# Seven-product blocks in a two-layer decoder trunk: products combined in PSUM, the fourth weight sum from SBUF, none put off

## The chip, the cores and the metric

One core of one Trainium2 chip runs the whole program. The metric is device time in microseconds. The kernel before took 1740.78 us (median of 3 runs, 1734.89 to 1745.19).

## What is computed

512 tokens of width 1024 pass two layers. Each layer computes, in float32:

```python
h = rms_norm(x, g)
proj = h @ w_in            # 7168 columns: pool, ret q/k, ret v, ret gate, mem q, 3 branch gates
merged = g_pool * (y_pool @ w_up_pool) + g_ret * (y_ret @ w_up_ret) + g_mem * (y_mem @ w_up_mem)
x = x + merged @ w_out
h2 = rms_norm(x, g2)
x = x + square(relu(h2 @ w_mlp1)) @ w_mlp2      # 1024 -> 4096 -> 1024
```

Between `proj` and `merged` stand three mixers: a causal pooling mixer, a retention with four heads in chunks of 128 tokens, and an attention to 256 memory tokens. After the second layer follows a last `rms_norm`.

## The kernel before, in words

**Precision.** Every operand is split into a high and a low part in fp32r: ScalarE casts (`wh`, `xh`), VectorE subtracts (`wl`, `xl`). Each matrix product is three matmuls, high by high, high by low, low by high (`mm`, lines 119 to 125). Weights are split by `split_w` (L114 ScalarE, L117 VectorE), into four buffers of each kind.

**Sections.** The large matrices are cut to blocks of 1024 x 1024, 16 per layer. One call of `products` is one section: a block in 2 x 2 quarters of 512, by the Strassen-Winograd scheme with seven products in place of eight. Operand quarters are `x.q[i, j]` (i: half of the tokens or columns, j: half of the contraction), results are (0,0), (0,1), (1,1) and (1,0). Before, the order is 1, 2, 5, 3, 6, 7, 4. Products 1 and 2 give (0,0); (0,1) needs 1, 5, 6 and 3; (1,1) needs 1, 5, 6 and 7; (1,0) needs 1, 6, 7 and 4 (signs left out). Each product has two halves of the contraction, `kp` 0 and 1, called units here: 24 matmuls of 256 columns each where the result is stored features first (`fm`), 12 of 512 columns else.

**Sums.** Sums of operand quarters are made by VectorE (`Operand.value`, L267) and split (`Operand.get`, L104 and L105). Sums of weight quarters are made by DMA: `Weight.take` splits a raw buffer, then GpSimd adds the next quarter from HBM to it (L225, accumulating). Buffer A holds w00, then + w01, then + w11, then + w10; buffer C holds w10, and buffer B holds w11, then + w01. So 6 loads and 8 accumulating DMAs of 512 KB make one section's weights. Eight raw tiles are shared.

**Order.** `push` prepares a unit (weight split, operand parts) and issues the matmuls of the unit three places before (`LOOK`). After each unit `settle` runs what is due: the function `after` of the product that ended (results out of PSUM, `done` for the sections that store, `acc` for those that add to x at L1183), operand parts in `wanted`, and one step of each side task (`advance`: norms, transposes, retention, pooling, attention). TensorE's order is as issued; the other engines are ordered by a scheduler, which `urgent` overrides. `until` goes on with the queue, and with empty steps after it, until a side task has what the next section needs.

**The put-off product.** In all sections but those called with `last=True` (w_out and the layer's last MLP block), product 4 is kept in `late` and issued by `owed` in the next section, after that section's product 1, accumulating on product 7's banks. So result (1,0) comes out two products into the next section. Product 2 then accumulates on product 1's banks, whose contents ScalarE has copied to `u` (L346).

**The layer's end.** `flush` and `drain` stand inside the loop over layers: at the end of layer 0 the queue and the side tasks are emptied before the next layer's first unit is prepared.

Of the kernel before, what the change touches and what calls it, by code (L numbers as in the profile page):

```python
# [13 lines left out]
ALU = mybir.AluOpType  # L14
# [11 lines left out]
NT = T // P  # L26
# [42 lines left out]
def tile_trunk(ctx, tc, a, out):  # L69
# [71 lines left out]
    wanted = []  # L141

    def settle():

        nonlocal post
        if post:
            f, post = post, None
            f()
        for w in list(wanted):
            x, p, kp = w  # L150
            if x.have(p, kp):
                x.get(p, kp)
                wanted.remove(w)
        advance()
# [37 lines left out]
    class Weight:  # L192
# [21 lines left out]
        def take(self, p, kp, between=None):  # L214
# [5 lines left out]
            part, then = {1: ("A", q(0, 1)), 5: ("A", q(1, 1)), 6: ("A", q(1, 0)), 4: ("A", None),  # L220
# [22 lines left out]
    class Operand:  # L243
# [12 lines left out]
        def value(self, p, kp):  # L256
# [4 lines left out]
            if (p, kp) not in self.sums:  # L261
                x, y, op = {5: lambda: (q[1, 0], q[1, 1], ALU.subtract),
                            6: lambda: (self.value(5, kp), q[0, 0], ALU.subtract),
                            7: lambda: (q[0, 0], q[1, 0], ALU.subtract),
                            3: lambda: (q[0, 1], self.value(6, kp), ALU.add)}[p]()
# [12 lines left out]
    late = []  # L278
    early = {}

    def owed():
        while late:
            late.pop(0)()

    def products(x, done, fm=False, last=False, acc=None, ahead=None):
# [15 lines left out]
        follows = {1: 2, 2: 5, 5: 3, 3: 6, 6: 7, 7: 4}  # L301

        def prep(p, kp, w=w):
            def f():
                wp = w.take(p, kp)
                for q in (p or 1, follows.get(p)):
                    if q and x.have(q, kp):
                        x.get(q, kp)
# [7 lines left out]
        def go(p, kp, into, new, fm=fm, then=None):  # L316
            def f(wp):
# [17 lines left out]
                if kp == n - 1:  # L335
                    return lambda: urgent(after, p, into) if last and p == 4 else after(p, into)
# [3 lines left out]
        def after(p, into):  # L340
            v = nc.vector.tensor_tensor
            bs = range(2)
            if p == 1:
                for b in bs:
                    sb["u", b] = slot(name="u2")
                    nc.scalar.copy(sb["u", b], ps[1][b])  # L346
            elif p == 2:
                for b in bs:
                    if acc:
                        if into == 2:  # L350
                            acc(0, 0, b, sb["u", b], ALU.add, False)
                        acc(0, 0, b, ps[into][b], ALU.add, True)
                    elif into == 1:
                        done(0, 0, b, ps[1][b], True)
                    else:
                        c = slot(name="c11")
                        v(c, sb["u", b], ps[2][b], ALU.add)
                        done(0, 0, b, c, False)
            elif p == 5 and acc and last:
                for b in bs:  # L360
                    sb["v", b] = slot(name="vv")
# [927 lines left out]
```

## Time and profile before

| | |
|---|---|
| median of 3 runs | 1740.78 us |
| the profiled execution | 1739.72 us |
| its span, first to last instruction | 1737.9 us |
| mean granted TensorE clock | 0.975 |
| TensorE busy | 1638.8 us (94%) |
| VectorE busy | 1329.6 us (77%) |
| ScalarE busy | 949.1 us (55%) |
| GpSimd busy | 332.1 us (19%) |
| read from HBM | 288.56 MB |

The profile gives busy times of each engine, the share of the TensorE clock that was granted, and what ended each idle time. A clock of 1.00 is 2.4 GHz and of 0.5 is 1.2 GHz. Matmuls overlap, and their ends are modelled: the pitch from one start to the next tells more than the duration of one.

### The profile page before, as it was taken

To read this page: it belongs to the slowest core of one execution; us is meant where nothing else is said; L and a number is where in the kernel's file an instruction comes from. 1 tells how busy PE (TensorE), PEld (TensorE's weight loads), DVE (VectorE), ACT (ScalarE), POOL (GpSimd) and SP (SyncE) were. 2 spreads that over 40 slices of the span, in tenths; PEclk is the share of its full clock that TensorE was granted. 3 is DMA by queue.
4 is the path that set the end of the run, shared out by engine and by line. 5 is a ranking of instruction groups with operands and counts; after the bars stand their busy time and mean duration, and the time that the engine had idled before them with its cause. 6 is when DMAs were issued, how large, how long until landed. Compare 5 with 4: busy or idle time off the path is not lost. (4 is left out here: it accounts for less than half of the span.)

```text
span 1737.9 us, 24766 instructions
## 1 busy us (share of the span) xinstructions
PE 1638.8 (94%) x9354; PEld 1430.2 (82%) x9354; DVE 1329.6 (77%) x1833; ACT 949.1 (55%) x1463; POOL 332.1 (19%) x292
## 2 busy tenths in 40 slices
PE   6899998999998999999979999999999899999996
PEld 5797887988878897979769888889788797979794
DVE  4898674876698878787887786758667988786878
ACT  6445664555266645455663457645544565545563
POOL 2122202200012212222121222021001122222221
PEclk9999998999999999999989999999999899999998
DMA  9699985963667978889789999767455778888874
GB/s 267 143 218 261 233 218 107 189 187 111 187 137 152 188 177 170 178 173 188 180 183 203 221 262 223 202 122 176 144 167 141 167 148 191 193 164 179 174 136 101
DMA packets 163449, 311.17 MB, mean 179 GB/s; under 512 B 11320, under 2 KB 12544, under 8 KB 163328
## 3 DMA queue, kind: packets, MB, share of 16 engines
q0 software_dynamic: 69632, 134.23, 46.6%
q1 hardware_dynamic: 83872, 159.42, 28.1%
q10 hardware_dynamic: 9824, 15.93, 2.6%
q8 instruction: 73, 1.20, 0.3%
q14 instruction: 48, 0.39, 0.1%
HBM read 288.56 MB, written 16.78 MB: 176 GB/s over the span
## 5 line engine op out<-in xcount | busy, mean ns | idle before, releaser
L114 ACT CAST wh<-raw 128x1024 fp32r<-128x1024 f32 x496 | 519.6, 1050 | 600.6 <-PE P L125 192.8
L117 DVE TENSOR_TENSOR wl<-raw,wh 128x1024 fp32r<-128x1024 f32 x496 | 605.6, 1224 | 284.8 <-ACT wh L114 283.4
L225 POOL DMA_DIRECT2D raw<-in_w_mlp x124 | 149.8, 1210 | 473.7 <-DVE wl L117 455.3
L225 POOL DMA_DIRECT2D raw<-in_w_in x108 | 131.3, 1216 | 454.3 <-DVE wl L117 340.8
L123 PE MATMUL P<-wh,x3h 128*128 128x512 f32 x160 | 68.7, 430 | 15.1 <-ACT x3h L104 15.0
L125 PE MATMUL P<-wh,x3l 128*128 128x512 f32 x160 | 69.1, 432 | 8.9 <-DVE x3l L105 8.9
L225 POOL DMA_DIRECT2D raw<-in_w_out x16 | 19.3, 1207 | 295.3 <-DVE wl L117 282.7
L1183 DVE TENSOR_TENSOR x<-x,P 128x512 f32<-128x512 f32 x104 | 68.4, 684 | 6.6 <-PE P L125 6.1
L124 PE MATMUL P<-wl,x3h 128*128 128x512 f32 x160 | 67.0, 419 | 1.9 <-DVE wl L117 1.9
L124 PE MATMUL P<-wl,x4h 128*128 128x512 f32 x160 | 64.2, 402 | 3.9 <-DVE wl L117 3.9
L123 PE MATMUL P<-wh,x1h 128*128 128x512 f32 x160 | 64.7, 404 | 1.7 <-ACT x1h L104 1.7
L125 PE MATMUL P<-wh,x5l 128*128 128x512 f32 x160 | 65.1, 407 | 0.6 <-DVE x5l L105 0.6
L123 PE MATMUL P<-wh,x4h 128*128 128x512 f32 x160 | 64.1, 401 | 1.1 <-ACT wh L114 1.1
L123 PE MATMUL P<-wh,x5h 128*128 128x512 f32 x160 | 63.2, 395 | 1.7 <-ACT x5h L104 1.7
L124 PE MATMUL P<-wl,x1h 128*128 128x512 f32 x160 | 63.9, 400 | 0.0
L125 PE MATMUL P<-wh,x1l 128*128 128x512 f32 x160 | 63.7, 398 | 0.0
L125 PE MATMUL P<-wh,x4l 128*128 128x512 f32 x160 | 63.5, 397 | 0.0
L123 PE MATMUL P<-wh,x2h 128*128 128x512 f32 x160 | 63.2, 395 | 0.0
L124 PE MATMUL P<-wl,x6h 128*128 128x512 f32 x160 | 62.5, 391 | 0.6 <-DVE wl L117 0.6
L124 PE MATMUL P<-wl,x5h 128*128 128x512 f32 x160 | 63.0, 394 | 0.0
L124 PE MATMUL P<-wl,x7h 128*128 128x512 f32 x160 | 62.6, 391 | 0.4 <-DVE wl L117 0.4
L124 PE MATMUL P<-wl,x2h 128*128 128x512 f32 x160 | 62.9, 393 | 0.0
(331 smaller groups left out, 5140.8 us busy)
## 6 DMA issues: line engine op xcount, KB each, us to landing
raw<-in_w_mlp POOLq DMA_DIRECT2D x128, 512.0 KB, 6.5
raw<-in_w_in POOLq DMA_DIRECT2D x112, 512.0 KB, 6.8
raw<-in_w_mlp SPq DMA_DIRECT2D x100, 512.0 KB, 4.6
raw<-in_w_in SPq DMA_DIRECT2D x88, 512.0 KB, 4.9
sgl<-sig SPq DMA_DIRECT2D x48, 256.0 KB, 5.8
raw<-in_w_mem_kv SPq DMA_DIRECT2D x16, 512.0 KB, 4.9
raw<-in_w_up_ret SPq DMA_DIRECT2D x16, 512.0 KB, 4.6
raw<-in_w_out POOLq DMA_DIRECT2D x16, 512.0 KB, 6.6
```

Source lines behind the costliest of these rows:

```text
L114: nc.scalar.copy(hi, raw)
L117: nc.vector.tensor_tensor(lw, raw, hi.bitcast(F32), ALU.subtract)
L123: nc.tensor.matmul(ps, sh, mh, start=start, stop=False, skip_group_check=True)
L124: nc.tensor.matmul(ps, sh, ml, start=False, stop=False, skip_group_check=True)
L125: nc.tensor.matmul(ps, sl, mh, start=False, stop=stop, skip_group_check=True)
L225: nc.gpsimd.dma_start(raw, rows2(then, kp), accum_op=ALU.add)
L1183: nc.vector.tensor_tensor(x, x, part, op)
```

## The change

Order and combination: the order is now 1, 2, 5, 3, 6, 4, 7. After product 5 ScalarE copies its two banks onto those of product 2. Product 6 accumulates on product 5's banks, VectorE then subtracts `u` there, product 4 accumulates on the copy in product 2's banks, product 7 on product 5's. No product goes to the next section, and `late`, `owed` are gone; signs of three operand sums are turned. Weights: buffer A ends with three terms, and the fourth sum is buffer C plus buffer A, both in SBUF. The loads move: A after product 2, C after product 6. `flush` and `drain` come once, at the end of the program. Some side tasks take other numbers of steps.

```diff
+    follows = {1: 2, 2: 5, 5: 3, 3: 6, 6: 4, 4: 7}
...
-        for w in list(wanted):
-            x, p, kp = w
-            if x.have(p, kp):
-                x.get(p, kp)
-                wanted.remove(w)
+        had = [w for w in wanted if w[0].have(*w[1:])]
+        for w in had:
+            w[0].get(*w[1:])
+            wanted.remove(w)
+        for x, p, kp in had:
+            q = follows.get(p)
+            if q and x.have(q, kp):
+                x.get(q, kp)
...
-            part, then = {1: ("A", q(0, 1)), 5: ("A", q(1, 1)), 6: ("A", q(1, 0)), 4: ("A", None),
+            part, then = {1: ("A", q(0, 1)), 5: ("A", q(1, 1)), 6: ("A", None), 4: ("C", None),
                           3: ("B", q(0, 1)), 7: ("B", None), 2: ("C", None)}[p]
...
+            if (p, kp) in ((3, 1), (6, 0)):
+                k = 0 if p == 3 else 1
+                nc.gpsimd.dma_start(self.buf["C"][k], self.buf["A"][k], accum_op=ALU.add)
...
-                    return lambda: urgent(after, p, into) if last and p == 4 else after(p, into)
+                    return lambda: urgent(after, p) if p in (5, 6) or (last if p == 7 else not acc if p == 2 else False) else after(p)
...
+            elif p == 2 and acc:
+                for b in bs:
+                    acc(0, 0, b, ps[2][b], ALU.add, False)
+                for b in bs:
+                    acc(0, 0, b, sb["u", b], ALU.add, True)
...
+            elif p == 5:
                 for b in bs:
+                    nc.scalar.copy(ps[2][b], ps[5][b])
             elif p == 3 and acc:
                 for b in bs:
                     acc(0, 1, b, ps[3][b], ALU.add, False)
+                    if last:
+                        acc(0, 1, b, sb["u", b], ALU.subtract, False)
+            elif p == 6:
                 if last:
                     for b in bs:
+                        acc(0, 1, b, ps[5][b], ALU.add, True)
                 for b in bs:
+                    v(ps[5][b], ps[5][b], sb["u", b], ALU.subtract)
+                if acc and not last:
+                    for b in bs:
+                        acc(0, 1, b, ps[5][b], ALU.add, True)
+                elif not acc:
+                    cs = [slot(name="c12") for _ in bs]
+                    for b in bs:
+                        nc.scalar.copy(cs[b], ps[5][b])
+                    for b in bs:
+                        v(cs[b], cs[b], ps[3][b], ALU.add)
+                    for b in bs:
+                        done(0, 1, b, cs[b], False)
+            elif p == 4 and acc:
                 for b in bs:
+                    acc(1, 0, b, ps[2][b], ALU.add, False)
+            elif p == 7 and acc:
+                for i, op in ((1, ALU.add), (0, ALU.subtract)):
+                    for b in bs:
+                        acc(1, i, b, ps[5][b], op, True)
+            elif p == 7:
+                cs = [slot(name="c21") for _ in bs]
                 for b in bs:
+                    nc.scalar.copy(cs[b], ps[5][b])
                 for b in bs:
+                    v(cs[b], ps[2][b], cs[b], ALU.subtract)
                 for b in bs:
+                    done(1, 1, b, ps[5][b], True)
                 for b in bs:
+                    done(1, 0, b, cs[b], False)
...
+        if ahead:
+            product_ahead(*ahead)
+        product(2)
+        if nxt:
+            nxt.load("A")
         product(5)
         product(3)
-        product(6)
-        product(7)
+        product(6, 5)
+        if nxt:
+            nxt.load("C")
+        product(4, 2)
+        product(7, 5)
         if nxt:
             nxt.load("B")
-        if last:
-            product(4)
-        else:
-            late.append(lambda: product(4, 7))
...
-                transposed(x, i, c, kp, lambda t, c: xn[t % 2, c], g, eng=nc.vector if kp else None)
+                transposed(x, i, c, kp, lambda t, c: xn[t % 2, c], g)
...
-            vs = []
+            vs = [split(v[0][hp], name="vs")]
+            yield
+            yield
             for t in range(NT):
-                vs.append(split(v[t][hp], name="vs"))
-                yield
+                if t + 1 < NT:
+                    vs.append(split(v[t + 1][hp], name="vs"))
                 yield
                 yield
...
+            if h == 0:
+                yield
+                yield
...
-            yield
+            for _ in range(3):
+                yield
...
-        flush()
-        drain()
+    flush()
+    drain()
```

## Rows read from the trace of the kernel before

**Rows 1.** The page, busy time of each engine.

```profile
PE 1638.8 (94%) x9354; PEld 1430.2 (82%) x9354; DVE 1329.6 (77%) x1833; ACT 949.1 (55%) x1463; POOL 332.1 (19%) x292
```

**Rows 2.** The view of cores: span and mean granted clock.

```profile
core 0: 1737.9 us, clock 0.975
```

**Rows 3.** Waits of TensorE, whole span: us in total, times, longest us.

```profile
PE P L123 <- ACT x3h L104: 18.2, 11, 1.9
PE tr L475 <- ACT xn L608: 17.4, 3, 9.0
...
PE y L123 <- ACT vsh L104: 8.7, 5, 2.9
```

**Rows 4.** Windows, product 3 of eight w_mlp2 sections: us, PE, PEld, DVE, ACT, POOL, PEclk.

```profile
1525.00:1542.00 17.00, 14.35 (x52) 10.14 (x51) 15.38 (x22) 7.53 (x10) 4.81 (x4) 0.90 1.08 187
1609.00:1624.00 15.00, 12.34 (x50) 8.62 (x49) 14.26 (x20) 7.32 (x10) 4.82 (x4) 1.00 1.07 175
...
sum 132.00, PE 110.53 PEld 77.38 DVE 119.95 ACT 62.68 POOL 38.62; mean PE 13.82 PEld 9.67 DVE 14.99 ACT 7.83 POOL 4.83
```

**Rows 5.** Timeline of TensorE, first matmuls of products: start us, us, instruction.

```profile
861.04 0.39 PE L123 MATMUL P<-wh,x7h 128*128 128x512 f32 x1
...
866.48 0.39 PE L123 MATMUL P<-wh,x4h 128*128 128x512 f32 x1
...
1531.68 0.50 PE L123 MATMUL P<-wh,x3h 128*128 128x512 f32 x1
...
1542.25 0.39 PE L123 MATMUL P<-wh,x6h 128*128 128x512 f32 x1
```

**Rows 6.** Windows at the other losses, same columns.

```profile
869.00:889.00 20.00, 11.03 (x58) 9.69 (x57) 15.73 (x25) 11.51 (x26) 4.65 (x5) 0.74 0.75 185
...
515.00:535.00 20.00, 14.27 (x67) 11.98 (x66) 18.88 (x31) 11.16 (x24) 3.89 (x4) 0.83 0.60 141
553.00:564.00 11.00, 8.46 (x65) 7.79 (x65) 9.79 (x14) 7.08 (x11) 3.74 (x4) 1.00 1.02 170
1368.00:1388.00 20.00, 14.52 (x64) 12.14 (x63) 18.66 (x30) 10.27 (x21) 3.92 (x4) 0.74 0.66 163
...
270.00:290.00 20.00, 15.13 (x71) 12.96 (x70) 5.77 (x10) 9.04 (x26) 2.07 (x3) 0.74 0.34 83
1122.00:1142.00 20.00, 15.01 (x78) 12.94 (x77) 6.14 (x10) 9.96 (x28) 2.40 (x4) 0.83 0.37 90
...
366.00:391.00 25.00, 22.18 (x128) 18.83 (x127) 17.46 (x36) 13.04 (x28) 0.00 (x0) 1.00 0.55 195
...
0.00:61.00 61.00, 42.44 (x181) 33.69 (x182) 33.27 (x47) 34.56 (x61) 14.43 (x18) 0.92 0.93 234
...
1725.00:1737.90 12.90, 0.44 (x2) 0.01 (x1) 7.97 (x15) 2.78 (x8) 0.69 (x1) 0.67 0.25 94
```

**Rows 7.** Timeline of VectorE behind the put-off product 4.

```profile
1521.71 1.22 DVE L117 TENSOR_TENSOR wl<-raw,wh 128x1024 fp32r<-128x1024 f32 x1
1522.84 0.69 DVE L1199 SCALAR_TENSOR_TENSOR u<-u 128x512 f32<-128x512 f32 x1
1523.44 0.69 DVE L267 TENSOR_TENSOR xs<-u,vv 128x512 f32<-128x512 f32 x1
```

**Rows 8.** Window of one w_mlp2 section, same columns.

```profile
1509.10:1547.70 38.60, 35.95 (x170) 28.97 (x169) 32.06 (x42) 22.43 (x32) 7.23 (x6) 0.96 0.86 176
```

**Rows 9.** Lines, by cost: instruction xcount | busy us, mean ns of one.

```profile
L117 DVE TENSOR_TENSOR wl<-raw,wh 128x1024 fp32r<-128x1024 f32 x496 | 605.6, 1224 | 284.8 <-ACT wh L114 283.4
L114 ACT CAST wh<-raw 128x1024 fp32r<-128x1024 f32 x496 | 519.6, 1050 | 600.6 <-PE P L125 192.8 <-PE P L124 190.5 <-PE up L125 72.7
...
L1183 DVE TENSOR_TENSOR x<-x,P 128x512 f32<-128x512 f32 x104 | 68.4, 684 | 6.6 <-PE P L125 6.1
...
L346 ACT COPY u<-P 128x512 f32<-128x512 f32 x56 | 30.6, 584 | 3.2 <-PE P L125 3.2
```

**Rows 10.** Accumulating weight DMAs (L225), from issue to landing.

```profile
DMA to landing us min/median/max: 5.8/6.6/11.3
```

More of the change, by code (lines that the diff above doesn't have):

```diff
@@ L307, in f @@
                     if q and x.have(q, kp):
-                        x.get(q, kp)
+                        for k in range(kp + 1):
+                            if x.have(q, k):
+                                x.get(q, k)
                     elif q == (p or 1):
@@ L443, in products @@
             w.skip()
-            product(2)
-            owed()
-            if nxt:
-                nxt.load("A")
         else:
             product(1)
-            own = not late and not ahead
-            if ahead:
-                product_ahead(*ahead)
-            owed()
-            if nxt:
-                nxt.load("A")
-            product(2, None if own else 1)
+        if ahead:
[3 more added lines that the diff above has]
+            nxt.load("A")
+        product(5)
+        product(3)
+        product(6, 5)
         if nxt:
             nxt.load("C")
-        product(5)
-        product(3)
-        product(6)
-        product(7)
+        product(4, 2)
+        product(7, 5)
         if nxt:
             nxt.load("B")
-        if last:
-            product(4)
-        else:
-            late.append(lambda: product(4, 7))
     def transposed(x, i, j, kp, src, gain=None, eng=None):
@@ L1112, in pooling @@
                 dp = split(s, name="dp")
-                yield
-                yield
-                yield
+                for _ in range(4):
+                    yield
                 ps = bank("pm")
@@ L1191, in tile_trunk @@
         products(gop, None, last=True, acc=add_to_x(
-            rows2nd, lambda i: start_side(rows2nd.operand(i, h2, gain("norm_mlp_g", l), 4 + i))))
+            rows2nd, lambda i: start_side(rows2nd.operand(i, h2, gain("norm_mlp_g", l), 4))))
         def relu2(act):
@@ L1219, in save, with end @@
                         yield
-            def end(i):
+            def end(i, l=l, rows=rows, hop=hop):
                 sides.append(save(i))
-                start_side(rows.operand(i, hop, gain("norm_mix_g", l + 1), 4 + i))
+                start_side(rows.operand(i, hop, gain("norm_mix_g", l + 1), 4))
         else:
@@ L1227, in tile_trunk, with end @@
                 nc.scalar.dma_start(gB[c], a["final_norm_g"].unsqueeze(0)[:, c * T:(c + 1) * T].broadcast_to([P, T]))
-            def end(i):
+            def end(i, l=l, rows=rows, hop=hop):
                 r = rows.factors(i)
```

80 lines of the change are left out of this document (11 added, 69 removed).

## The prediction, made before the change was run

> **What bounds the kernel now.** The page comes first: TensorE is busy 1638.8 us [rows 1] of a span of 1737.9 us at a mean granted clock of 0.975 [rows 2]. So 99.1 us are idle, and the clock takes 2.5% of the span, 43.4 us: 142.5 us that a change which leaves the matmuls alone can win. No matmul is added or removed here, so everything hangs on these 142.5 us. The waits of TensorE then say who ends them [rows 3]: the operand of product 3, the scaled rows of a norm, the split values of the retention. Windows put them in time. "Loss" below is idle time of TensorE in a window plus the window times (1 - PEclk); a clock that fell to its lower level, 1.2 GHz, does so behind such an idle time.
>
> - Product 3 in the eight w_mlp2 sections: the windows sum to 132.00 us with 110.53 busy, 21.5 idle; six of the eight have PEclk 0.90 over 17 us, two 1.00 [rows 4], another 10.2. That is 31.7 us, but short gaps hide under modelled ends. Start to start, an undisturbed product takes 866.48 - 861.04 = 5.44 us, and product 3 took 1542.25 - 1531.68 = 10.57 [rows 5], 5.1 lost, where the window of the same place gives 2.65 + 1.7 = 4.35. Scaled by 5.1/4.35: **37 us**.
> - The end of layer 0 (869 to 889): 8.97 idle, and 5.2 of clock: **14.2**.
> - w_out and the start of the MLP, both layers: 5.73 + 3.4, then 5.48 + 5.2, and 2.54 at product 3 of the first w_mlp1, twice (the second layer's window is alike): **24.9**.
> - The retention's last chunks, both layers: 4.87 + 5.2 and 4.99 + 3.4: **18.5**.
> - Attention's first scores: 2.8 in layer 0, taken as 3.7 for the mean of both layers: **7.4**.
> - The first 61 us: 18.6 + 4.9: **23.4**. The last 12.9 us: **12.5**. These five are from [rows 6].
>
> The sum is 138 of 142.5 us: the account closes, and no other place matters.
>
> **The change part by part.**
>
> *No product is put off.* Before, result (1,0) of w_mlp1 leaves PSUM only behind the next section's product 1 and product 4. VectorE makes the squared relu at 1522.84 and the first sum for product 5 at 1523.44 [rows 7], 8.2 us before product 3 starts [rows 5]. In these 8.2 us, or 10.9 to product 3's second unit, VectorE has ten operations of 512 columns (sums and low parts for 5, 6 and 3), four weight splits and two additions to x. Operations in a row start 0.60 us apart, a split takes 1.13 [rows 7]: 12 x 0.60 + 4 x 1.13 = 11.7 us, with ScalarE's casts between them. It does not fit, hence the stall. After, all results are out at the end of product 7, and products 1, 2 and 5 (3 x 5.44 = 16.3 us) run before product 3; its second unit needs its parts after 19.0 us. VectorE's work there: four operations that end the section before, the same ten, six splits, four additions to x: 18 x 0.60 + 6 x 1.13 = 17.6 us, and the additions are issued last. It fits with 1.4 us to spare, and 3.8 if the additions wait. VectorE is busy 32.06 of 38.6 us in such a section [rows 8], so its work flows over little. I leave 6 of 37 us: **-31**.
>
> *`flush` and `drain` leave the loop.* At the end of layer 0 TensorE waits 9.0 us for the second token half's scaled rows [rows 3], because `drain` puts their transposes ahead of the next layer's product 1. After, only the first half must be there; the second is due behind product 1, and a product of the next block computed ahead covers it. A place like this exists: w_out's end, where the queue isn't emptied. I leave 4 us: **-10**.
>
> *w_out and the start of the MLP.* The sections called with `last` lose VectorE work: 24 combining operations become 18, and of those between product 6's end and the norm six go (6 x 0.68 = 4.1 us by [rows 9]). The norm's copies from the transposes move from VectorE to ScalarE, the second half is due one step earlier. w_out's product 4 may still wait for weights. I leave 9 of 24.9: **-16**.
>
> *Retention.* Before, each value split stands three steps ahead of its use, 12 steps per pair of heads; after it is 10, and the rotated q and k are complete two units earlier. The last chunk comes six units earlier and the one before five, so both lie inside the memory projection instead of behind it. I leave 2.5 of 18.5: **-16**.
>
> *Attention and pooling.* Two steps before the first scores end that wait. But head and group take more steps (6 for 4 per head, 4 for 3 per group): pooling then ends five empty steps behind w_up_ret, where TensorE has nothing but attention's transposes and products. I price that at the wait that it replaces, less 1 per layer: **-2**. *The start*: ScalarE takes VectorE's copies, **-3** of 23.4. *The tail*: VectorE has 6 fewer combining operations in front of the last norm, **-3** of 12.5, as 6 x 0.60 = 3.6 is the most.
>
> *Costed at nothing.* Storing sections go from 10 VectorE and 2 ScalarE combining operations to 8 and 8, 22 sections; 6 x 0.58 us of ScalarE [rows 9] in 38 to 41 us, with ScalarE busy 55% [rows 1]. It is covered by ScalarE's idle time; without cover it would be 3.5 us per section. The accumulating sections that aren't last go from 18 VectorE operations to 16 and two copies. SP's loads: C moves behind product 6, six units (16.3 us) ahead of its use, longer than the slowest landing of any accumulating DMA, 11.3 us [rows 10]. On GpSimd's queue the number of issues stays at eight; behind an addition of A to C that waits at its head stand the next section's first weight sum and the norm's small power. Behind a ScalarE cast of product 4's weights that waits for the addition stand copies and casts for products 7 and the next 1, all due two products later. GpSimd is busy 19%.
>
> *The addition in SBUF* has no row. Below: 5.8, the quickest landing from HBM; above: 11.3, the slowest [rows 10]. I take the median, 6.6: the same size on the same queue. Its time matters only beyond a point (rival 1). A gain lies in it too, two HBM reads fewer per section; but none of the losses above is a wait for weights from HBM of more than a few us, so it ends at 5.
>
> *New waits in PSUM.* Product 6 may start only when ScalarE has copied product 5's banks, with product 3 between, 5.44 us for 1.2 us of copies. Product 7 may start only when VectorE has subtracted `u`, and the result has been read: in an accumulating section four operations, 4 x 0.68 = 2.7, behind at most two splits already queued, 2.4: 5.1 of the 5.44 us of product 4. Nothing below; above 2.5 us in each of 10 accumulating sections and 1 in the 22 others, 47. Since every one has its cover by the rows I take 8: **+8**. Sections whose first product was computed ahead lose two units of cover for their weight sums: **+2**.
>
> **Sum**: -31 - 10 - 16 - 16 - 2 - 3 - 3 + 8 + 2 = -71. The profiled execution took 1739.72 us, 1.06 below the median. 1739.7 - 71 = 1668.7, **1668 us**.
>
> **The rivals.**
>
> 1. *Slower: the addition in SBUF lands too late.* From product 5's start the split of 6's first unit begins at 2.72 us, when a buffer comes free, and ends 1.05 + 1.22 later [rows 9], at 5.0; then the addition issues. Product 4's second unit starts seven units after product 5, at 19.0, and needs 2.3 for its split. So 11.7 us are allowed. The landings from HBM keep this, the longest barely [rows 10]; against it, both ends of this one are in SBUF, where the operand traffic is. At 15 us each section stalls 3.3 us, 32 x 3.3 = 106: 1774 us. It decides from 11.7 + 71/32 = 13.9 us. Chance 0.07.
> 2. *The banks wait.* The products that depend on a bank that another engine has just written stall by the upper bound, 47 in place of 8: 1707 us. For it: VectorE's 83% in w_mlp2; against: two to four short operations with a product's time for each. The Trainium skill (Perfetto Trace Analysis, Optimizing Tensor Performance, Matmuls) says that independent groups should rotate through PSUM banks, so that the evacuation of one overlaps the matmuls of the next; this change does the reverse, and that is this rival's rule. No row before shows such a dependence. Chance 0.16.
> 3. *The lateness moves.* The 1.4 us to spare is gone to VectorE's order, and product 3 (or 4) waits as before: 1668 + 31 = 1699. Chance 0.10.
> 4. *It doesn't do what it says*: where the stalls come from the scheduler's order and not from the put-off product, only the layer's end is won: 1730. Chance 0.05.
>
> **How the numbers follow.** My forecast (1634 to 1692, terms off by half at most) has 0.62. The range takes in rivals 2 and 3: 1634 to 1712. A measurement here can tell 0.5%, 8.7 us, from no change. Rivals 1 (and a little for several small losses together) give slower 0.08; half of rival 4 gives same 0.05; the rest is faster, 0.87.
>
> **What would show it.** The waits on x3h fall from 18.2 to under 4; no wait of 9 us at the layer's end; y's waits on vsh under 2; the mean clock rises to 0.985 or more; the additions in SBUF land within 11 us. Wrong: idle time of TensorE ended by ScalarE's copy or VectorE's subtraction on P banks in most sections, or by wl at product 4.

## The result, and the profile after

The changed kernel takes 1723.65 us in the median of 5 runs (1722.77 to 1727.91), the kernel before 1740.77 (5 runs): a ratio of 0.9909, 95% interval 0.9885 to 0.9934. It is faster, by 17 us where 71 were forecast; 1723.65 lies above the range of 1634 to 1712. The profiled execution of the changed kernel spans 1720.8 us. Ratios below are to the kernel before, run on the same chip beside it; differences from the changed kernel are worked out from two ratios times 1740.8.

The page and the view of cores, against [rows 1, 2]:

```profile
PE 1623.3 (94%) x9354; PEld 1422.6 (83%) x9354; DVE 1260.9 (73%) x1723; ACT 1030.4 (60%) x1651; POOL 317.4 (18%) x292
```
```profile
core 0: 1720.8 us, clock 0.979
```

VectorE has lost 68.7 us of work, ScalarE got 81.3 more. But the granted clock rose from 0.975 to 0.979 only, not to 0.985: TensorE still runs into gaps, and in the windows around the norms, below, it was granted 0.80 to 0.94. In w_mlp2, where product 3 had its gaps before, they are gone. First matmuls of products 3 and 6 of a w_mlp2 section, in the timeline of TensorE (start us, us, instruction):

```profile
1522.98 0.39 PE L123 MATMUL P<-wh,x3h 128*128 128x512 f32 x1
...
1528.42 0.39 PE L123 MATMUL P<-wh,x6h 128*128 128x512 f32 x1
```

1528.42 - 1522.98 = 5.44 us, against 10.57 [rows 5], and 5.44 in all eight such sections. The same two products in the first w_mlp1 section, which follows a norm:

```profile
556.12 0.28 PE L123 MATMUL P<-x3h,wh 128*128 128x256 f32 x1
...
560.70 0.38 PE L123 MATMUL P<-x3h,wh 128*128 128x256 f32 x1 [1.36 <-ACT x3h L104]
...
562.04 0.39 PE L124 MATMUL P<-x3l,wh 128*128 128x256 f32 x1 [0.96 <-DVE x3l L105]
...
570.01 0.58 PE L123 MATMUL P<-x6h,wh 128*128 128x256 f32 x1 [4.95 <-ACT P L362]
```

Here product 3 takes 570.01 - 556.12 = 13.9 us, where an undisturbed one of this kind takes 5.76. The bracket at a row's end is the idle time of the engine and what ended it: the operand's cast, its low part, and then ScalarE's copy of product 5's bank. TensorE's waits over the whole span, against [rows 3] (us in total, times, longest):

```profile
PE tr L447 <- ACT xn L579: 23.1, 5, 8.2
PE P L123 <- ACT P L362: 12.4, 3, 5.3
PE gps L537 <- DMA grows<-in_pool_scale: 11.6, 1, 11.6
...
PE P L123 <- ACT x3h L104: 3.9, 3, 1.7
PE P L124 <- DVE wl L117: 3.5, 4, 1.0
```

x3h fell from 18.2 to 3.9, none of it in w_mlp2. In its place stand the scaled rows of the norms (five waits for three), the copy of product 5's banks, and the transpose of the norms' gains at the start. Windows at these places, against [rows 6]:

```profile
222.00:242.00 20.00, 16.81 (x88) 14.00 (x87) 16.01 (x29) 13.60 (x25) 1.56 (x3) 1.00 0.93 251
...
500.00:532.00 32.00, 24.25 (x100) 18.15 (x99) 26.21 (x39) 20.94 (x36) 5.28 (x5) 0.89 0.77 191
556.00:574.00 18.00, 10.74 (x69) 10.00 (x68) 11.23 (x16) 10.31 (x17) 2.17 (x2) 0.81 0.95 228
853.00:883.00 30.00, 23.60 (x130) 19.98 (x129) 20.97 (x31) 21.38 (x40) 6.87 (x6) 0.94 0.87 216
895.00:912.00 17.00, 12.56 (x39) 8.91 (x38) 11.71 (x17) 8.21 (x13) 2.13 (x2) 0.80 0.98 237
1345.00:1376.00 31.00, 24.16 (x97) 18.09 (x96) 25.54 (x38) 19.43 (x34) 4.96 (x5) 0.89 0.75 187
1400.00:1418.00 18.00, 11.77 (x79) 11.24 (x78) 11.86 (x17) 11.13 (x19) 2.13 (x2) 0.81 0.85 209
1708.00:1720.80 12.80, 0.41 (x2) 0.00 (x0) 7.92 (x14) 2.56 (x8) 0.69 (x1) 0.60 0.42 164
```

Losses reckoned as in the prediction, idle time plus window times (1 - PEclk); the tail by its idle time alone, as there:

| place | before | after | change | forecast |
|---|---|---|---|---|
| product 3 in w_mlp2 (0 after), with new waits for weights and operands of products 4, 5 and 7 in these sections | 37 | 6.8 | -30 | -31 |
| w_out and start of the MLP, both layers: 11.3 + 10.7 + 10.3 + 9.7 | 24.9 | 41.9 | +17 | -16 |
| end of layer 0, start of layer 1: 8.2 + 7.8 | 14.2 | 16.0 | +2 | -10 |
| retention: 3.2 + 2.8 | 18.5 | 6.0 | -12.5 | -16 |
| attention, four windows | 7.4 | 10.3 | +3 | -2 |
| start, by the start of the first product 6 (60.5, 65.9) | | | +5 | -3 |
| tail | 12.5 | 12.4 | 0 | -3 |
| PSUM waits and sections whose first product is computed ahead | | in the rows above | | +10 |

The sum is some -16, the measured gain 17: the account closes. Of the missing 54 us, 45 belong to the three stretches around a norm (17 + 16, 2 + 10), and 8 to the start, whose first section follows a norm as well.

### The profile page after: what moved, and what is told of

Same layout as the page of the kernel before. It is cut to its first block, busy times and chain, and to the rows that moved or that the text cites. A ratio compares the mean times of both kernels' runs of the same rounds, so it can differ in the third digit from the quotient of the medians.

```text
span 1720.8 us, 24865 instructions
## 1 busy us (share of the span) xinstructions
PE 1623.3 (94%) x9354; PEld 1422.6 (83%) x9354; DVE 1260.9 (73%) x1723; ACT 1030.4 (60%) x1651; POOL 317.4 (18%) x292
## 4 chain that ended last, share of the span: by engine, by line
PE 52%; issue 23%; DMA 10%; DVE 5%; POOL 5%; ACT 4%; SPq 0%; ACTq 0%; POOLq 0%; DVEq 0%
PE P L125 12%; PE P L123 12%; PE P L124 12%; DMA raw<-in_w_mlp 5%; POOL raw L229 4%; DMA raw<-raw 3%; PE up L125 3%; PE up L123 3%; PE up L124 3%; DMA raw<-in_w_in 2%; ACT wh L114 2%; DVE wl L117 2%; DVE x L1161 1%; PE kv L123 1%; PE kv L124 1%
## 5 line engine op out<-in xcount | busy, mean ns | idle before, releaser
L229 POOL DMA_DIRECT2D raw<-in_w_mlp x92 | 122.1, 1359 | 392.9 <-DVE wl L117 260.4
L229 POOL DMA_DIRECT2D raw<-in_w_in x80 | 106.1, 1366 | 315.7 <-DVE wl L117 271.7
L232 POOL DMA_DIRECT2D raw<-raw x64 | 57.7, 901 | 170.0 <-DMA raw<-in_w_mlp 70.1
L1161 DVE TENSOR_TENSOR x<-x,P 128x512 f32<-128x512 f32 x120 | 78.1, 679 | 1.6 <-PE P L125 1.6
L123 PE MATMUL P<-wh,x6h 128*128 128x512 f32 x160 | 64.3, 402 | 5.2 <-ACT x6h L104 3.0
L229 POOL DMA_DIRECT2D raw<-in_w_out x12 | 15.9, 1462 | 282.6 <-DVE wl L117 282.6
L125 PE MATMUL P<-wh,x7l 128*128 128x512 f32 x160 | 63.7, 398 | 3.0 <-DVE x7l L105 3.0
L123 PE MATMUL P<-x6h,wh 128*128 128x256 f32 x192 | 56.4, 294 | 10.2 <-ACT P L362 10.2
L123 PE MATMUL P<-wh,x7h 128*128 128x512 f32 x160 | 64.7, 404 | 0.1
L125 PE MATMUL P<-wh,x3l 128*128 128x512 f32 x160 | 63.8, 399 | 0.6 <-DVE x3l L105 0.6
L125 PE MATMUL P<-wh,x6l 128*128 128x512 f32 x160 | 63.7, 398 | 0.5 <-DVE x6l L105 0.5
```

The lines of the kernel that those rows point to most:

```text
L123: nc.tensor.matmul(ps, sh, mh, start=start, stop=False, skip_group_check=True)
L125: nc.tensor.matmul(ps, sl, mh, start=False, stop=stop, skip_group_check=True)
L232: nc.gpsimd.dma_start(self.buf["C"][k], self.buf["A"][k], accum_op=ALU.add)
L1161: nc.vector.tensor_tensor(x, x, part, op)
```

## The experiments

The first theory came from GpSimd's queue in the first w_mlp1 section of the changed kernel. L229 are the sums from HBM, L232 the additions of A to C; each section has two of these, one per unit:

```profile
542.73 1.23 POOL L229 DMA_DIRECT2D raw<-in_w_mlp  x1 [7.96 <-DVE wl L117]
550.98 0.90 POOL L232 DMA_DIRECT2D raw<-raw  x1 [7.02 <-DMA raw<-in_w_mlp]
551.55 2.79 POOL L229 DMA_DIRECT2D raw<-in_w_mlp  x2
559.27 0.92 POOL L232 DMA_DIRECT2D raw<-raw  x1 [4.93 <-DMA raw<-in_w_mlp]
560.04 1.40 POOL L229 DMA_DIRECT2D raw<-in_w_mlp  x1
```

The addition for C's first unit waits 7.02 us at the head of the queue for A's first unit to land, and the sum for A's second unit, which comes earlier in the program, stands behind it until 551.55. ScalarE, whose instructions also run one behind the other, shows what follows:

```profile
559.09 1.04 ACT L114 CAST wh<-raw 128x1024 fp32r<-128x1024 f32 x1 [4.15 <-DMA raw<-in_w_mlp]
560.04 0.61 ACT L104 CAST x3h<-xs 128x512 fp32r<-128x512 f32 x1
...
565.82 1.04 ACT L114 CAST wh<-raw 128x1024 fp32r<-128x1024 f32 x1 [2.22 <-DMA raw<-raw]
566.78 0.61 ACT L104 CAST x4h<-q 128x512 fp32r<-128x512 f32 x1
567.29 1.15 ACT L1180 ACTIVATE c<-c 128x512 f32<-128x512 f32 x2
568.35 1.13 ACT L1181 ACTIVATE c<-c 128x512 f32<-128x512 f32 x2
569.39 1.05 ACT L362 COPY P<-P 128x512 f32<-128x512 f32 x2
```

A cast waits for that late sum, and the operand of product 3 stands behind it; a cast of product 4's weights waits for the second addition, and behind it and four activations stands the copy that product 6 needs. Such an order is rare. By the timeline of GpSimd over the whole span, in six of the 32 sections two sums from HBM are issued between the two additions, in the others one at most. The six are the start's section, w_out's two, and the three first sections behind a norm.

(In the variants below, line numbers shift by a few. In the diffs, `...` marks a cut, and the names of runs behind `#` are added.)

| run | edit to the changed kernel | us | ratio, 95% interval |
|---|---|---|---|
| e1 | all accumulating DMAs in traced order | 1764.9 | 1.0150 (1.0125 to 1.0174) |
| e2 | product 5's copies on VectorE | 1727.8 | 0.9920 (0.9902 to 0.9938) |
| e3 | step counts of attention, pooling as before | 1747.2 | 1.0039 (1.0021 to 1.0056) |
| e5 | flush and drain in the loop | 1724.0 | 0.9891 (0.9875 to 0.9908) |
| e4 | norm's copies split as before | 1720.4 | 0.9895 (0.9876 to 0.9913) |
| e6 | gains' transpose later | 1730.3 | 0.9953 (0.9936 to 0.9970) |
| e7 | product 3's additions to x urgent | 1725.6 | 0.9923 (0.9902 to 0.9944) |
| e8 | fourth sum from HBM, as before | 1783.6 | 1.0265 (1.0240 to 1.0290) |
| e9 | copies on VectorE behind norms only | 1725.9 | 0.9931 (0.9918 to 0.9945) |
| e10 | norm's transposes a step later | 1725.8 | 0.9917 (0.9894 to 0.9941) |
| e11 | e9 and e10 | 1731.0 | 0.9956 (0.9939 to 0.9973) |
| e12 | gain rows loaded by SyncE | 1729.8 | 0.9946 (0.9933 to 0.9958) |
| e13 | no addition of A to C (product 4 lacks its weight sum) | 1681.1 | 0.9666 (0.9649 to 0.9684) |
| e14 | no copy of product 5's banks | 1719.3 | 0.9882 (0.9865 to 0.9899) |
| e15 | order edges on GpSimd and ScalarE | 1711.6 | 0.9842 (0.9827 to 0.9857) |
| e16 | order edge on GpSimd alone | 1705.6 | 0.9804 (0.9786 to 0.9822) |
| e17 | e16, addition as a GpSimd operation | 1760.6 | 1.0117 (1.0097 to 1.0137) |
| e18 | e16 and e4 | 1705.8 | 0.9793 (0.9768 to 0.9818) |

**e1: the sums in their traced order.**

```diff
+    def add_dma(dst, src):
...
+        with tc.issue_after(last_add):
+            d = nc.gpsimd.dma_start(dst, src, accum_op=ALU.add)
+        last_add = d.ins
```

All accumulating weight DMAs go through it.

> The changed kernel with one edit: each accumulating weight DMA is issued on GpSimd behind the one traced before it, so that the addition of A to C no longer goes ahead of the sum for A's second unit and of the sums for B. Queue theory (what was lost is lost because that addition waits 5 to 9 us at the head of GpSimd's queue, and ScalarE's in-order casts wait behind the sums it holds up): TensorE's wait for the gains' rows falls from 11.6 us to under 4, its waits for ScalarE's copy of product 5's banks from 12.4 to under 6, the time from 1723.7 to 1700 to 1712. Source theory (an addition with both ends in SBUF slows all weight DMAs, whatever its place in the queue): 1719 to 1728, landings as before. Bank theory (product 6's wait for the copied bank is a cost of the dependence itself): 1719 to 1728, and the 12.4 us stay.

42 us slower than the changed kernel. A's second sum did go first, but now both additions of a section are issued behind both sums of B, at most 2.7 us apart; and they land later. Timeline of GpSimd of e1, same section (product 3 starts at 568.07), then the DMA issues of e1 (count, KB each, median us to landing):

```profile
559.30 1.20 POOL L204 DMA_DIRECT2D raw<-in_w_mlp  x1 [3.39 <-DVE wl L117]
562.22 1.20 POOL L204 DMA_DIRECT2D raw<-in_w_mlp  x1 [1.72 <-DVE wl L117]
565.07 1.22 POOL L204 DMA_DIRECT2D raw<-in_w_mlp  x1 [1.65 <-DVE wl L117]
565.80 2.32 POOL L204 DMA_DIRECT2D raw<-raw  x2
```
```profile
raw<-raw POOLq DMA_DIRECT2D x64, 512.0 KB, 10.1
```

10.1 us for 6.6 in the changed kernel. The loss lies elsewhere than expected: the six sections named above take as long as in the changed kernel, while product 6 takes 7.6 to 10.5 us in the eight w_mlp2 sections (5.4 to 5.8 in the changed kernel). TensorE waits for its operand x6h (14.5 us in 10 waits, eight of them in these sections, for 3.0 in 2). In the section from 684 us on that operand's cast stands behind a weight cast that waits 4.45 us for an addition. The queue theory in this form fell; what it left is that a few us of lateness of these additions cost much.

**e2, e9: product 5's copies on VectorE**, in all sections, and only in the four behind a norm.

```diff
-                    nc.scalar.copy(ps[2][b], ps[5][b])
+                    nc.vector.tensor_copy(ps[2][b], ps[5][b])       # e2
+                    (nc.vector.tensor_copy if ahead else nc.scalar.copy)(ps[2][b], ps[5][b])       # e9
```

> The changed kernel with product 5's two banks copied by VectorE in place of ScalarE. Queue theory: ScalarE is what was held up, so TensorE's 12.4 us behind that copy go to under 3, against 72 more operations (some 45 us) on VectorE: 1712 to 1722. Bank theory: product 6 waits as long behind VectorE's copy, 10 us or more, 1720 to 1728. A third case: VectorE's added work brings the waits of w_mlp2 back, 1728 or more.

> The changed kernel with product 5's copy on VectorE in the four sections that follow a norm alone (those with a product computed ahead), on ScalarE elsewhere. Copy theory (product 6 waits 5.1, 2.3 and 5.4 us there because ScalarE reaches the copy only behind a weight cast that waits for a sum, and behind four activations): the three waits fall to 2 to 2.5 us each as in the run with all copies on VectorE, with the low clock behind them 10 to 13 us in all: 1710 to 1715. Rival (the copy has to wait for VectorE's reading of bank 2 anyway, and the wait stays on another instruction): 1720 to 1726.

TensorE's wait at the copy fell from 12.4 to 6.1 us in e2 and 3.9 in e9, and neither is faster. TensorE's waits for VectorE's wl rose from 3.5 to 11.6 and 8.1 us. Curing this wait by itself wins nothing.

**e3: old step counts.**

```diff
-            for _ in range(3):            # attention
-                yield
+            yield
...
-                for _ in range(4):        # pooling
+                for _ in range(3):
```

> The changed kernel with the step counts of attention and pooling as before (one step in place of three ahead of the probabilities' transposes, three in place of four ahead of pooling's product; the two steps ahead of the first scores stay). If the added steps made the attention stretch 7 us worse (empty steps at its end), 1714 to 1720. If they were needed (the transposes then wait for the scaled probabilities), 1722 to 1732, with a longer wait of TensorE for pr.

22.6 us slower: the added steps were needed. Part of it shows as TensorE's wait for the scaled probabilities `pr`, which rises from 4.0 us to:

```profile
PE pt L1039 <- ACT pr L1032: 11.4, 6, 3.6
```

**e5: flush and drain back in the loop.**

> The changed kernel with flush and drain back inside the loop over layers. If moving them out is what saved the 9 us wait at the layer's end, that wait returns: 1728 to 1736. If it only moved the wait (the stretch from 850 to 912 us lost 18.6 us in the changed kernel, 12.4 in the kernel before), 1716 to 1722.

1724.0: no difference. The transposes wait for scaled rows once more (27.1 us in 6 waits for 23.1 in 5), but layer 1's first section then has no wait for the copy (9.4 us in 2 waits over the span, for 12.4 in 3). Moving `flush` and `drain` out only moved the loss.

**e4, e6, e7, e10, e12: one wait at a time.**

```diff
-                transposed(x, i, c, kp, lambda t, c: xn[t % 2, c], g)               # e4
+                transposed(x, i, c, kp, lambda t, c: xn[t % 2, c], g, eng=nc.vector if kp else None)
...
-        for _ in range(4):                # ahead of load_gains                     # e6
+        for _ in range(8):
...
-    ... urgent(after, p) if p in (5, 6) or (last if p == 7 else ...                 # e7
+    ... urgent(after, p) if p in (5, 6) or (last if p in (3, 7) else ...
...
-    ... gain("norm_mlp_g", l), 4) ...     # "norm_mix_g" alike                      # e10
+    ... gain("norm_mlp_g", l), 5 - i) ...
...
-            nc.scalar.dma_start(rest[o:o + src.shape[0], :], src)                   # e12
+            nc.sync.dma_start(rest[o:o + src.shape[0], :], src)
```

> The changed kernel with the norm's copies out of PSUM shared between ScalarE and VectorE as before (the second of each pair on VectorE). ScalarE theory (the two starts of the MLP and the start of layer 1 lose 10.0, 8.8 and 8.6 us because ScalarE, in order, has the norm's 16 more copies of 0.47 us ahead of operand casts and of product 5's bank copy): those three places fall by half together, 1708 to 1716. Rival (they wait for weight sums, and the copies only fill the time): within 4 us of 1723.7.

> The changed kernel with eight steps in place of four between the loads of the gain rows and their transpose. If TensorE's 11.8 us at the start are only that transpose standing in TensorE's order ahead of rows that ScalarE issues late, the wait goes and nothing takes its place: 1709 to 1715. If product 3 of the first section waits there anyway (its operands come through the same ScalarE queue), 1718 to 1724.

> The changed kernel with product 3's additions to x at high priority in the sections called with last (as product 6's are). If the norm's transposes wait 4.4, 6.0 and 4.4 us because these additions stand behind operand sums and weight splits on VectorE, these waits fall to under 2 us each: 1710 to 1717. If what holds them is ScalarE (the squares behind weight casts), within 4 us of 1723.7.

> The changed kernel with the first token half's transposes one step later, behind product 7's last unit instead of ahead of it, at the three places where a norm follows. Order theory (TensorE stands 4.4, 6.0 and 4.4 us at transposes while the last unit of product 7, 2.7 us, is ready behind them): that unit fills 2.7 us of each wait, and what its cover of the copies was worth is lost: 2 to 6 us faster in all, 1717 to 1722. Rival (the unit was the cover of the copies and casts for the next product 1, which now wait as long): within 2 us or slower, 1722 to 1730.

> The changed kernel with the four gain rows loaded by SyncE in place of ScalarE, the transpose at its place. The rows then land before the transpose, and TensorE's 11.8 us there go. In the run with the transpose later product 3 waited 6.2 us for x3h at the same place; if that is the limit, 4 to 6 us are won here and stay won, since the rotary tables aren't put off: 1717 to 1721. If the loads hold up weight loads on SyncE's queue, 1724 to 1730.

None is faster beyond its interval, and e6 is slower by 8 us. In e6 the gains' wait is gone, but x3h is waited for at the same place (6.0 us), and the retention's scores, which need the rotary tables built behind the gains, wait longer (7.5 us for 4.3). In e7 the additions to x do come earlier, but the transposes wait as long (23.1 us). In e10 the wait for scaled rows falls to 14.5 us, and x1h is waited for 21.2. In e12 the gains' transpose waits no less (12.9 us). e11 puts e9 and e10 together and takes 1731.0 us: there is no gain to add up.

> Both edits of the two runs before in one kernel. If they act at different places, their gains add: 1705 to 1712 with both theories right, 1718 to 1722 with the second alone. If the scheduler's order on ScalarE and VectorE shifts with each edit so that a gain at one place comes back at another, 1718 to 1728.

**e8: the fourth sum from HBM.**

```diff
-            part, then = {... 6: ("A", None), 4: ("C", None),
+            part, then = {... 6: ("A", q(1, 0)), 4: ("A", None),
...
-            if (p, kp) in ((3, 1), (6, 0)):
-                k = 0 if p == 3 else 1
-                nc.gpsimd.dma_start(self.buf["C"][k], self.buf["A"][k], accum_op=ALU.add)
```

> The changed kernel with the fourth weight sum made as before: product 4's weights by adding a third quarter to A from HBM behind product 6's casts, and no addition of A to C. If the addition in SBUF is what costs (it waits at the head of GpSimd's queue for A to land, and product 4's cast waits for it in ScalarE's order), 1700 to 1714. If it is harmless, the later landing behind product 6's cast makes product 4 wait for weights, 1726 to 1760, with TensorE's waits for wl at product 4.

62 us slower than the changed kernel, 2.65% slower than the kernel before. TensorE's waits for weights, the low parts `wl` (16 of 18 at products 4 and 7) and the high parts `wh` (all at product 4):

```profile
PE P L124 <- DVE wl L117: 18.4, 18, 1.7
PE P L123 <- ACT wh L114: 8.0, 4, 3.8
```

In the new order product 4 directly follows product 6, so A's last sum has no product in between to land. These waits are part of the 62 us; TensorE's wait for the copy of product 5's banks also rises, from 12.4 to 20.0. Adding buffer A to C isn't a saving of HBM reads here: without it the new order loses more than it wins.

**e13, e14, e15, e16: landing, bank or order.**

```diff
-                nc.gpsimd.dma_start(self.buf["C"][k], self.buf["A"][k], accum_op=ALU.add)      # e13
...
-                    nc.scalar.copy(ps[2][b], ps[5][b])                                         # e14
...
+                d = nc.gpsimd.dma_start(raw, rows2(then, kp), accum_op=ALU.add)                # e15, e16
+                if p == 5:
+                    self.a1 = d.ins
...
+                with tc.issue_after(self.a1):                                                  # e15, e16
+                    nc.gpsimd.dma_start(self.buf["C"][k], self.buf["A"][k], accum_op=ALU.add)
...
+                if p == 4:                                                                     # e15
+                    with tc.issue_after(sb["copied"]):
+                        wp = w.take(p, kp)
```

`self.a1` is the sum for A's second unit, `sb["copied"]` ScalarE's copy of product 5's banks; e15 also puts the activations of result (0,0) behind that copy.

> The changed kernel without the addition of A to C: it leaves out the fourth weight sum, so that product 4 runs with a quarter in place of the sum. Landing theory (behind a norm the chain cast, sum of A, addition to C, cast is too long for ScalarE's and VectorE's order, and what is cured at one place is paid at the next): with nothing to wait for, the 48 us of losses between each product 6 ahead of a norm and the first product 6 behind it fall by half or more: 1685 to 1703. Rival (VectorE's and ScalarE's work behind a norm, not the landing, sets these stretches): 1715 to 1724.

> The changed kernel without the copy of product 5's banks (it leaves the copy out, so that product 4 accumulates on product 2's result). Bank theory (the dependence of product 6 on another engine's reading of its bank is a cost of its own): TensorE's 12.4 us behind the copy and the low clock behind them go and stay gone: 1703 to 1712. Landing theory: the 12.4 us go, and the wait passes to the next operand or weight behind the same casts (x6h, wl of product 4): 1715 to 1724.

> The changed kernel with two orders written out: on GpSimd the first addition of A to C is issued behind the sum for A's second unit (and no later); on ScalarE product 4's weight casts and the activations of the first result are issued behind the copies of product 5's banks. Order theory (TensorE's waits for the copy, 12.4 us, and for x3h, 3.9, come from those two queues' orders alone): 1703 to 1712. Landing theory: the casts for product 4 come later by as much, and 1716 to 1728.

> The first of these two orders alone, on GpSimd. In the run with all sums in their traced order the additions of A to C were issued in pairs and landed after 10.1 us in the median, where they took 6.6 in the changed kernel. If that pairing is what made that run 41 us slower, this one, which moves only the first of each pair and by 2 to 5 us, is within 6 us of the changed kernel, 1718 to 1730, with additions landing in 6 to 8 us; if any delay of these additions costs as much, 1735 or more.

e13 gives the size: without the addition the kernel takes 1681.1 us, 42 less, and its clock is 0.986. That is the addition with all that it brings: its place in the queue, its own landing, and its traffic (the loads of w_mlp and w_in land after 4.5 and 4.7 us in the median, for 5.2 in the changed kernel). Without the copy (e14) the time is 5 us less, and the intervals overlap; there the waits passed to x3h (9.3 us) and x5h (7.3). e16, one edge on GpSimd, wins 18 us. In it no section has more than one sum from HBM between its two additions. First matmuls of products 3 and 6 in the first w_mlp1 section, of e13, then of e16:

```profile
543.69 0.28 PE L123 MATMUL P<-x3h,wh 128*128 128x256 f32 x1
...
554.15 0.39 PE L123 MATMUL P<-x6h,wh 128*128 128x256 f32 x1 [4.17 <-ACT P L359]
```
```profile
551.78 0.28 PE L123 MATMUL P<-x3h,wh 128*128 128x256 f32 x1
...
562.22 0.39 PE L123 MATMUL P<-x6h,wh 128*128 128x256 f32 x1 [4.15 <-ACT P L365]
```

Product 3 takes 10.5 us in e13 and 10.4 in e16, in place of 13.9: at this place one order edge gives back all that the addition cost. Each timeline of TensorE, cut at the first matmul of every product 2, shows where the profiled executions differ from the changed kernel's (us; the start reaches to the second section's product 2, and e1's profiled execution is 5 us above its median):

| | start | w_out, 2 sections | first behind a norm, 3 | w_mlp2, 8 | the other 18 | sum |
|---|---|---|---|---|---|---|
| e13 | -7.8 | -10.9 | -11.9 | -10.8 | -1.7 | -43 |
| e16 | -3.8 | -8.3 | -10.3 | +0.6 | +6.3 | -16 |
| e15 | -3.0 | -8.4 | -25.2 | +15.9 | +7.1 | -14 |
| e1 | +0.2 | -1.6 | +0.5 | +24.2 | +24.3 | +48 |

So e16 cures the six sections, and w_mlp2 keeps its loss: product 7 takes 6.4 to 6.8 us there in four sections of the changed kernel and in five of e16, but 5.44 in e13. No run says how the 24 us between e16 and e13 divide between landing, traffic and the wait for A. The timeline of GpSimd of e16, same section:

```profile
538.39 1.23 POOL L229 DMA_DIRECT2D raw<-in_w_mlp  x1 [7.95 <-DVE wl L117]
543.00 1.20 POOL L229 DMA_DIRECT2D raw<-in_w_mlp  x1 [3.38 <-DVE wl L117]
545.33 0.90 POOL L235 DMA_DIRECT2D raw<-raw  x1 [1.13 <-DMA raw<-in_w_mlp]
549.51 0.86 POOL L235 DMA_DIRECT2D raw<-raw  x1 [3.29 <-DMA raw<-in_w_mlp]
550.06 2.82 POOL L229 DMA_DIRECT2D raw<-in_w_mlp  x2
```

Counted from product 3's start, A's second sum goes 4.2 us earlier than in the changed kernel (8.8 ahead for 4.6), and the second addition 5.4 us earlier (2.3 ahead, for 3.1 behind). In e1 A's second sum was as early (8.8 ahead), but the additions went at 2.3 and 1.7 ahead, behind B's sums. So the queue theory was right about the six sections and e1 was the wrong cure: in e16 the sum goes ahead of the addition, and the addition ahead of B's sums. e15's second edge takes the copy's wait away (0.4 us for 12.4), and product 3 behind a norm takes 6.2 to 6.5 us; but product 5 of the first w_mlp2 section then takes 10.3 and 10.4 us in the two layers, waiting for its operand's cast (5.0 us in 2 waits), and the time is 6 us more than e16's. As the scheduler orders the other engines anew for every edit, e16's 18 us are that edge with what it does to their order.

**e17: the addition on GpSimd itself.**

```diff
-nc.gpsimd.dma_start(self.buf["C"][k], self.buf["A"][k], accum_op=ALU.add)
+nc.gpsimd.tensor_tensor(self.buf["C"][k], self.buf["C"][k], self.buf["A"][k], ALU.add)
```

> The kernel with the one order edge on GpSimd, and the addition of A to C made by GpSimd as an operation on 128x1024 in place of a DMA (128 operations of a length that no row shows). If the landing costs the 25 us between the order edge's run (1705.6) and the run without the addition (1681.1), an operation of up to 4 us gives most of it back: 1684 to 1698. If the wait for A at the head of the queue costs it, 1702 to 1710. If GpSimd's operation holds up the weight sums behind it, or VectorE beside it, as much as it saves, 1706 to 1730.

54 us slower than e16. In the mean the operation stays within the 4 us of the expectation, but VectorE stands still beside it: its weight splits take 43 us more than in e16 (645.2 for 602.5), and TensorE waits 20.5 us for x5l. Lines of GpSimd, its timeline, then VectorE's of e17:

```profile
L235 POOL TENSOR_TENSOR raw<-raw 128x1024 f32<-128x1024 f32 x64 | 188.1, 2940 | 80.3 <-issue 65.2 <-DMA raw<-in_w_in 14.3 <-POOL raw L235 0.7
```
```profile
615.51 3.36 POOL L235 TENSOR_TENSOR raw<-raw 128x1024 f32<-128x1024 f32 x1 [1.97 <-issue]
```
```profile
614.84 0.68 DVE L1164 TENSOR_TENSOR x<-x,P 128x512 f32<-128x512 f32 x1
615.44 1.22 DVE L117 TENSOR_TENSOR wl<-raw,wh 128x1024 fp32r<-128x1024 f32 x1
616.57 2.84 DVE L105 TENSOR_TENSOR x5l<-xs,x5h 128x512 fp32r<-128x512 f32 x1
```

A 512-column operation that takes 0.68 us elsewhere lasts 2.84, to half a us past the end of GpSimd's (618.87). (e17 runs 64 operations, not the 128 that its expectation names.)

**e18: the order edge and the norm's copies split.**

> The kernel with the order edge on GpSimd, and the norm's copies out of PSUM shared between ScalarE and VectorE as in the kernel before. If ScalarE's queue is what is left at the starts of the MLP (three waits of 4.2 us or less for product 5's copy, and the low clock behind them), 1695 to 1702. If VectorE, busy without a gap in these stretches, takes up as much as ScalarE gives, 1703 to 1710.

1705.8, no different from e16. Both are faster than the two kernels that the prediction compared; e16 is the simpler one.

## Why the prediction was wrong

*Right:* the diagnosis of w_mlp2. The put-off product was what made product 3 wait, and all eight stalls are gone. That the term came out so close (-30 for -31) is in part chance: the 6 us left over were meant for product 3, which lost nothing, and the 6.8 that stand are waits of products 4, 5 and 7 that I hadn't named (1.3 in e13, so most of them are the addition's). The retention's -12.5 and the closing account also stand. The landing of the addition was sized well, 4.6 to 11.1 us, median 6.6, where 6.6 was taken; as that came from sums with an HBM source, which in the changed kernel took 7.6, the exact fit is luck.

*The step that failed* is "costed at nothing", its part on GpSimd's queue: behind an addition of A to C that waits at its head were to stand only the next section's first weight sum and the norm's small power, and behind the cast that waits for it on ScalarE only work due two products later. The view of L232 in the changed kernel shows what it waited for (us, times):

```profile
  DMA raw<-in_w_mlp: 70.1, 28
  DMA raw<-in_w_in: 66.6, 25
  DMA raw<-in_w_out: 23.7, 4
```

160 us at the head of the queue, in 57 of 64 additions. I gave the addition 11.7 us, from 5.0 us behind product 5's start on, and asked only whether it lands in that time; I didn't ask when A itself lands, for which the same queue must wait first, nor which sums of the same section wait behind. In the first w_mlp1 section product 5 starts at 550.36 and the second addition issues at 559.27, 8.9 us later instead of 5.0; its cast starts at 565.82, 15.5 us behind product 5's start, still inside the 16.7 that I had reckoned for product 4. But by then A's second sum, product 3's operand and product 5's copy had been held up in the two queues. In most sections this order doesn't arise, and the loss is at most 1 to 3 us each, at product 7 in w_mlp2 above all. In w_out, at the start and behind a norm it does, and there the norm's copies and squares stand in ScalarE's queue as well. Why the order built ahead of the run puts the addition first at just these places isn't shown. Priced by e13, the addition cost 42 us against nothing, 31 of them in these six sections and 11 in w_mlp2; 18 of the 42 are won back by the one order edge. The forecast less its error is 1668 + 42 = 1710, 14 below the result.

The rest lies in terms that I sized by hope. Around the norms and at the start 53 us are missing by the account; e13 gives back 31 of them, and 22 remain. *flush and drain*, -10: e5 shows 0; I named the second half's transposes as covered and left out that the first section of layer 1 gets the same queues as the MLP's. *w_out and the start of the MLP*, -16: fewer VectorE operations and ScalarE copies were to help; e4 undoes the copies at no cost. Even in e13 TensorE waits 22.4 us for scaled rows in 5 waits and 10.5 for the copy in 3, as in e16 (22.9, 10.5): this part isn't the addition. That ScalarE's and VectorE's orders behind a norm cause it is argued from e9, e10 and e15, where the wait moved with each edit (e15: -25 us behind the norms, +16 in w_mlp2); no run removed it. *Attention*, -2: measured +3, though the added steps of attention and pooling are worth 22.6 us against the old counts in the new kernel (e3). *Start*, -3: +5; without the addition it is 7.8 us shorter, and its gains' wait 4.3 us for 11.6.

*The rivals.* What came is nearest to the first, that the addition lands too late, but not as it was written: at landings of 6.6 us, not from 13.9 on, and most of it in six sections, since what the addition waits for and holds up counts too. It cost 42 us, where its price was 106 for all 32 sections, and so the sign stayed that of the forecast. The second, the banks, was priced at 47 us for 8; the copy's waits show 12.4 us, and leaving the copy out changed the time by 5, not clear of the intervals. The Trainium skill (Perfetto Trace Analysis, Optimizing Tensor Performance, Matmuls) asks that independent matmul groups rotate through PSUM banks; that breaking this rule cost something here is not shown, and e14's 5 us are about a tenth of what I gave it.

*The signs named in advance:* the waits on x3h fell under 4 us and the retention's wait for `vsh` is no longer among TensorE's waits; landings stayed within 11 us in all but one of 64 (11.1); the wait at the layer's end fell from 9.0 to 5.8 us, and the clock reached 0.979, not 0.985. "Idle time ended by ScalarE's copy" came in three sections, not in most.

## What to carry to other kernels

When a change puts a new transfer on an in-order queue, ask first what it waits for at the head and which instruction of the same section stands behind it; its landing time alone says little. Where the same lateness shows as a wait on a cast, a copy and a transpose, leave out the suspected source for one run before curing the waits one by one: here seven such cures (e2, e4, e6, e7, e9, e10, e12) were worth nothing, and one order edge at the source 18 us. Then look at every section, not only at the one in which the wait first showed: what e1 lost, it lost in sections that had run well. A part that seems a saving on the side may be what carries the rest: undo each part alone (e8: 62 us).

## What was not expected of the hardware

Accumulating DMAs between SBUF buffers, 512 KB each, landed after 6.6 us in the median in the changed kernel, 7.5 in e16 and 10.1 in e1, where two of them are issued within 2.7 us and right behind two sums from HBM. Pairs less than 1 us apart took no longer there (10.4) than the others (10.1); what makes them late isn't separated.

GpSimd's addition of 128x1024 takes 2.94 us in the mean of e17, and a VectorE operation with two SBUF inputs beside it lasts until it ends (2.84 us for 0.68), while the additions to x with one input in PSUM keep 0.68 in the mean. The Trainium skill (SBUF — State Buffer, SBUF: two separate sides) says that a VectorE operation with two SBUF inputs and a GpSimd operation that reads SBUF take a shared pair of ports by turns, each for its whole length; e17's trace agrees, with these two durations.
